# Moving each set of split activations to its own distance from the weights in the 512-byte block

## The chip, the cores and the metric

One core of one Trainium2 chip runs the whole program. The metric is the device time of one execution in microseconds (us); shorter is better.

## What is computed

Two transformer blocks over 256 tokens of width 1024, in float32. The first: a modulated norm, a mixer (retention heads and differential attention over the tokens and 256 context tokens), and a feed-forward layer that picks 16 single-neuron experts out of 16384 for each of 8 heads. The second: a short convolution mixer, attention to 256 memory tokens, a gated feed-forward layer (2 x 2816 columns up, 2816 rows down), shared keys and values, block attention, attention to memory again, a second feed-forward layer, and a last norm. Cut to the order of the second block:

```python
x = x + short_conv_mixer(h, conv_w_in[l], conv_w[l], conv_w_out[l])       # layer 0
x = x + moba_attention(h, moba_w_q[j], moba_w_o[j], cos, sin, k_blk, ...) # layer 1
x = x + mem_cross_attention(rms_norm_2(x, norm_mem[l]), ...)              # both layers
x = x + swiglu(rms_norm_2(x, norm_ffn[l]), ffn_w_gu[l], ffn_w_down[l])    # both layers
```

Nearly all of the work is products of the 256 tokens with large weight matrices that are each read once from memory.

## The kernel before, in words

**Tiles.** Activations lie transposed: 128 partitions hold 128 of the 1024 columns, a tile has 8 chunks (k) of 256 tokens, so 1024 bytes a chunk and partition. A weight block is 128 x 1024 float32, 512 bytes for each of eight 128 x 128 pieces. Every product of two float32 matrices is made of three float32r products: each factor is split into a high part and a low part (`whi`, `wlo` for weights in `split_w`, L113; `hh`, `hl` and their like for activations), and `mm3` (L134) multiplies high by high, low by high and high by low. For one output of 128 x 256 that is a run of 24 matmuls: eight pieces of `whi` with the high activations, eight of `wlo` with the high activations, eight of `whi` with the low activations. Before each matmul TensorE loads its 128 x 128 weights; the load of the next weights goes on while the matmul before streams its 256 tokens.

**Where things lie.** `placed` (L103) makes a tile with some room and returns a view that starts `at` elements into it. The values of `at` (16, 32, 40, 48) differ because the tiles start at different addresses. In the allocation of this kernel the three `whi` and two `wlo` buffers start at byte 224 of a 512-byte block, and so does every weight piece; all the sets that the change touches start at byte 416, which is 192 bytes further on, high and low alike. The memory sets (`hmh`, `hml` of `mem_kv`, L1001) of the second block's filler and the mixer's `hh`, `hl` (L455) are not made by `placed`: they start at byte 224, distance 0; the filler's set in the mixer starts at 256. In `mem_attn(0)` the turned probabilities `pTh`, `pTl` start at 384 and the memory values that are loaded for them at 256. Below, the distance of a matmul is the start of the operand that is streamed less the start of the operand that is loaded, modulo 512 bytes; where the activations are loaded and the weights streamed (`natural_steps`), 192 becomes 320.

**Stages.** `mixer` (0 to 288 us of the trace), then `peer`: 16 query blocks and 128 expert blocks with the set `h2h`, `h2l` (292 to 762), then the expert outputs (772 to 1120, with operands that the change leaves alone), then `conv_mixer`, `mem_attn(0)`, `swiglu(0)`, `moba`, `mem_attn(1)`, `swiglu(1)` and `finish`. SyncE's queue fetches the weight blocks in order, ScalarE makes the high part, VectorE or GpSimd the low part, TensorE multiplies; all orders are fixed when the program is built. Blocks of the filler (`fill` banks) are put between the blocks of other stages by hand (`PLACES`).

**Names.** `gained` (L264) makes a scaled set `hh`, `hl` for `mem_attn`, `conv_mixer`, `swiglu` and `moba`; `cat` is the set that a stage's last projection reads (`oh`/`ol`, `ch`/`cl`); `act` is `fh`/`fl`, 22 chunks; `hq` is moba's query set. The values in `moba` come from `natural_steps` (L166), where the activations are the loaded weights and the weights stream.

Of the kernel before, what the change touches and what calls it, by code (L numbers as in the profile page):

```python
# [28 lines left out]
KC = 8  # L29
EPS = 1e-6  # L30
NCH = 128
NKC_FF = 22
# [33 lines left out]
LOWEST = -3.0e38  # L66

ROOM = 128
G_NORM1, G_NORM2, G_MIX, G_MEM, G_MEMKV, G_FFN, G_KV, G_FINAL = 0, 1, 2, 4, 6, 8, 10, 11


class Build:
# [188 lines left out]
            nc.vector.scalar_tensor_tensor(h[1][:, k, cols], t, Bv[:, k:k + 1],  # L261
                                           h[0][:, k, cols].bitcast(F32), op0=OP.add, op1=OP.subtract)

    def gained(self, pool, x, gi, name="h", at=40):  # L264

        hi = self.placed(pool, name + "h", at, tag=name + "h", bufs=1)
        lo = self.placed(pool, name + "l", at, tag=name + "l", bufs=1)
        for k in range(KC):
            self.gain_chunk(x[:, k], gi, k, hi[:, k], lo[:, k])
        return hi, lo  # L270
# [441 lines left out]
    def peer(self):  # L712
        nc, io = self.nc, self.io
        with ExitStack() as ctx:
            self.banks(ctx, "peer")
            big = self.pool(ctx, "slots")
            pool = self.pool(ctx, "peer")
            slots = big.tile([P, NCH, T], F32, name="slots")
            h = self.placed(pool, "h2h", 48), self.placed(pool, "h2l", 48)
            space = slots[:, FREE:, :].rearrange("p c t -> p (c t)")  # L720
            at = [0]

# [190 lines left out]
            for cp in range(NCH // 2):  # L913
                self.lo_plan = UPLAN if cp < R1 else GPLAN
                o = self.psum([P, 2, T])
# [23 lines left out]
            pool = self.pool(ctx, "experts")  # L939
# [189 lines left out]
    def mem_attn(self, l, kv):  # L1129
        nc, io = self.nc, self.io  # L1130
        with ExitStack() as ctx:
            pool = self.pool(ctx, f"mem{l}")
            kT, v = kv
            h = self.gained(pool, self.x, G_MEM + l)
            cat = self.placed(pool, "oh", 40), self.placed(pool, "ol", 40)
            r = None

            def query(hd):
                nonlocal r
                o = self.psum([P, 2, T])  # L1140
                q = pool.tile([P, 2, T], F32, name="q", tag="q", bufs=1)
                qh, ql = (pool.tile([P, 2, T], F32R, name="q" + c, tag="q" + c, bufs=3) for c in "hl")
                for i in range(2):
                    self.block(o[:, i], io["mem_wq"][l, 2 * hd + i], h, late=hd == i == 0)
                if hd == 0:
                    r = self.tracked_norm(pool, "nr", tables=l == 0)
                nc.vector.scalar_tensor_tensor(q, o, 1.0 / 16.0, r[:, None, :].to_broadcast([P, 2, T]),
                                               op0=OP.mult, op1=OP.mult)
                nc.scalar.copy(qh, q)
                getattr(nc, QLO).tensor_sub(ql, q, qh)  # L1150
                return qh, ql

            def weigh(hd, q):
                ps = []
                for tt in range(2):
                    s = self.psum([P, T], "sc")
                    t = slice(tt * P, (tt + 1) * P)
                    self.mm3(s, [(q[0][:, i, t], q[1][:, i, t], kT[0][:, 2 * hd + i], kT[1][:, 2 * hd + i])
                                 for i in range(2)])
                    ps.append(self.softmax(pool, s, T, "ms"))  # L1160
                return ps

            def turned(ps):
                pT = [pool.tile([P, 2, 2, P], F32R, name="pT" + c, tag="pT" + c, bufs=2) for c in "hl"]
                for tt, p in enumerate(ps):
                    tr = self.psum([P, 2, P], "aux")
                    for j in range(2):
                        nc.tensor.transpose(tr[:, j], p[:, j * P:(j + 1) * P], self.ident)
                    nc.scalar.copy(pT[0][:, :, tt], tr)
                    nc.vector.tensor_sub(pT[1][:, :, tt], tr, pT[0][:, :, tt])  # L1170
                return pT

            def apply(hd, pT):
                o = self.psum([P, 2, T], "aux")
                for i in range(2):
                    c = slice((2 * hd + i) * P, (2 * hd + i + 1) * P)
                    self.mm3(o[:, i], [(v[0][:, j, c], v[1][:, j, c], pT[0][:, j], pT[1][:, j]) for j in range(2)])
                nc.scalar.copy(cat[0][:, 2 * hd:2 * hd + 2], o)
                nc.vector.tensor_sub(cat[1][:, 2 * hd:2 * hd + 2], o, cat[0][:, 2 * hd:2 * hd + 2])

            self.at(f"m{l}")
            qs = [query(0), query(1)]
            self.at(f"mq{l}")
            ps = weigh(0, qs[0])
            for hd in range(3):
                if hd < 2:
                    qs.append(query(hd + 2))
                self.at((f"mh{l}", hd))
                pT = turned(ps)
                ps = weigh(hd + 1, qs[hd + 1])  # L1190
                apply(hd, pT)
            self.at(f"me{l}")

            def rest():
                pT = turned(ps)
                yield
                apply(3, pT)

            self.residual_l(io["mem_wo"][l], cat, 6, rest())
# [27 lines left out]
    def conv_mixer(self, hook):  # L1227
        nc, io = self.nc, self.io
        with ExitStack() as ctx:
            pool = self.pool(ctx, "conv")  # L1230
            cw = self.load(pool, "conv_w", [P, KC, 3])
            h = self.gained(pool, self.x, G_MIX, at=16)
            cat = self.placed(pool, "ch", 16), self.placed(pool, "cl", 16)

            def gate(m, o, b):
                cu = pool.tile([P, 2, T], F32, name="cu", tag="cu", bufs=2)
                nc.vector.tensor_mul(cu, o, r[:, None, :].to_broadcast([P, 2, T]))
                z = pool.tile([P, T], F32, name="z", tag="z", bufs=2)
                nc.gpsimd.tensor_mul(z, cu[:, 0], cu[:, 1])
                y = pool.tile([P, T], F32, name="cy", tag="cy", bufs=2)  # L1240
                nc.vector.tensor_scalar(y, z, cw[:, m, 2:3], None, op0=OP.mult)
                nc.vector.scalar_tensor_tensor(y[:, 1:], z[:, :T - 1], cw[:, m, 1:2], y[:, 1:],
                                               op0=OP.mult, op1=OP.add)
                nc.vector.scalar_tensor_tensor(y[:, 2:], z[:, :T - 2], cw[:, m, 0:1], y[:, 2:],
                                               op0=OP.mult, op1=OP.add)
                nc.gpsimd.tensor_mul(y, y, r)
                t = pool.tile([P, T], F32, name="ct", tag="ct", bufs=2)
                nc.vector.tensor_mul(t, b, y)  # L1248
                nc.scalar.copy(cat[0][:, m], t)
                nc.vector.tensor_sub(cat[1][:, m], t, cat[0][:, m])  # L1250

            self.adder = getattr(nc, CADD)
            for k in range(KC):
                self.track(self.x[:, k], k)
            self.adder = nc.gpsimd
            for m in range(KC):
                self.at(("c", m))
                if m == HOOK:
                    hook()
                o = self.psum([P, 2, T], "sc" if m < 2 else "mm")  # L1260
                for i, c in enumerate((1, 2)):
                    self.block(o[:, i], io["conv_wi"][8 * c + m], h, late=m == i == 0)
                    if m == 1 and i == NORM1:
                        r = self.tracked_norm(pool, "nr", tables=True)
                b = self.psum([P, T])
                self.block(b, io["conv_wi"][m], h)
                if m == 0:
                    first = o, b
                    continue
                if m == 1:  # L1270
                    gate(0, *first)
                gate(m, o, b)
            self.at("ce")
            self.residual_l(io["conv_wo"], cat)

    def swiglu(self, l):
        nc, io = self.nc, self.io
        with ExitStack() as ctx:
            pool = self.pool(ctx, f"ffn{l}")
            h = self.gained(pool, self.x, G_FFN + l)  # L1280
            self.at(f"f{l}")
            act = self.placed(pool, "fh", 40, NKC_FF), self.placed(pool, "fl", 40, NKC_FF)
            for m in range(NKC_FF):
                o = self.psum([P, 2, T])
                for i in range(2):
# [12 lines left out]
            for m in range(KC):  # L1298
                o = self.psum([P, T])
                n = 0  # L1300
                while n < NKC_FF:
# [8 lines left out]
                    n = e  # L1310
# [33 lines left out]
    def moba(self):  # L1344
        nc, io = self.nc, self.io
        with ExitStack() as ctx:
            pool = self.pool(ctx, "moba")
            mask = self.load(pool, "causal", [P, 2, T])
            hk = self.gained(pool, self.x, G_KV)
            v = pool.tile([P, 2, 1024], F32, name="v")  # L1350
            r = rn = None
            waiting = []
# [28 lines left out]

            self.at("bk")
            kT = pool.tile([P, KC, T], F32, name="k")
            hq = [self.placed(pool, "hq" + c, 32) for c in "hl"]

            def query(hd):
                return plain(io["moba_wq"][hd], hq, 128.0 ** -0.5)
# [9 lines left out]
                ahead = t  # L1397
                self.gain_chunk(self.x[:, hd], G_MIX + 1, hd, hq[0][:, hd], hq[1][:, hd])

            cat = self.placed(pool, "oh", 32), self.placed(pool, "ol", 32)  # L1400

            def weigh(hd, q):
                ps = []
# [219 lines left out]
```

## Time and profile before

| | |
|---|---|
| median of 3 runs | 1889.74 us (1888.1 to 1890.78) |
| profiled execution | 1882.41 us, its span 1880.6 us |
| TensorE matmul busy | 1833.2 us, 97% of the span |
| VectorE, ScalarE, GpSimd busy | 70%, 52%, 24% |
| mean DMA rate | 178 GB/s |
| mean granted clock of TensorE | 0.992 |

The profile is that of one execution. Busy times of matmuls are modelled at their ends (a matmul's record is about 276 ns long although the next one starts after 113 ns), so the distance between starts is what counts: the chain in order of time gives a stretch and its matmuls, and the timeline gives the start of each run of eight.

### The profile page before, as it was taken

The numbers are of one execution on the slowest core, as the hardware profiler recorded it, in microseconds if no ns is written. First come the engines' busy times: TensorE is split into PE (matmuls) and PEld (weight loads), VectorE is DVE, ScalarE is ACT, GpSimd is POOL, SyncE is SP. The second block draws the span as 40 slices with busy tenths as digits, with TensorE's granted clock in tenths as the row PEclk, the third lists the DMA queues.
The fourth block names the chain that finished last, engine by engine and source line by source line (L and its number), as shares of the span: only waits on it lengthen the run. The fifth ranks groups of instructions, "written<-read, shape, count | busy, mean of one in ns | idle before, by whom it ended". The sixth has DMA issues, their size and how long they took to land.

```text
span 1880.6 us, 34809 instructions
## 1 busy us (share of the span) xinstructions
PE 1833.2 (97%) x13562; PEld 1717.2 (91%) x13562; DVE 1313.8 (70%) x2592; ACT 975.1 (52%) x1533; POOL 453.7 (24%) x254
## 2 busy tenths in 40 slices
PE   8999999999999999999999998999999999999997
PEld 6796888999999999788888878999999999999997
DVE  7879875995566676865555568777765679766654
ACT  7746335445555444445545555465554645555543
POOL 0001105787766777100000004112000111110001
PEclk9999999999999999999999999999999999999999
DMA  8763444454444444755555555544555553445553
GB/s 298 254 217 105 142 129 156 170 189 169 150 160 154 157 157 157 247 191 195 195 191 193 196 192 184 191 169 148 200 193 196 190 180 124 169 136 190 187 184 124
DMA packets 99765, 335.13 MB, mean 178 GB/s; under 512 B 12400, under 2 KB 13456, under 8 KB 99216
## 3 DMA queue, kind: packets, MB, share of 16 engines
q1 hardware_dynamic: 98160, 330.68, 51.0%
q8 instruction: 106, 1.74, 0.4%
q10 hardware_dynamic: 1440, 2.23, 0.3%
q14 instruction: 59, 0.48, 0.1%
HBM read 329.59 MB, written 3.28 MB: 177 GB/s over the span
## 4 chain that ended last, share of the span: by engine, by line
PE 87%; DVE 6%; DMA 3%; ACT 3%; issue 1%; POOL 0%; SPq 0%; DVEq 0%; ACTq 0%; POOLq 0%
PE mm L144 54%; PE pair L956 17%; PE mm L179 4%; PE pair L893 3%; PE fill L179 2%; DVE wlo L122 2%; PE fill L144 1%; PE sc L144 1%; DMA mraw<-w_mod 1%; PE aux L144 1%; DMA raw<-w_mod 1%; ACT whi L118 1%; DMA raw<-peer_v 0%; PE sc L628 0%; PE sc L554 0%
## 5 line engine op out<-in xcount | busy, mean ns | idle before, releaser
L118 ACT CAST whi<-raw 128x1024 fp32r<-128x1024 f32 x564 | 591.9, 1051 | 558.3 <-PE mm L144 280.4
L122 DVE TENSOR_TENSOR wlo<-raw,whi 128x1024 fp32r<-128x1024 f32 x420 | 526.7, 1255 | 298.7 <-PE pair L956 131.6
L122 POOL TENSOR_TENSOR wlo<-raw,whi 128x1024 fp32r<-128x1024 f32 x144 | 344.7, 2395 | 131.6 <-PE mm L144 113.6
L144 PE MATMUL mm<-hh,whi 128*128 128x256 f32 (+1 forms) x1184 | 178.2, 287 | 5.9 <-DVE ct L1248 5.1
L144 PE MATMUL mm<-hl,whi 128*128 128x256 f32 (+1 forms) x1184 | 174.5, 284 | 2.1 <-DVE hl L261 1.2
L144 PE MATMUL mm<-hh,wlo 128*128 128x256 f32 (+1 forms) x1184 | 175.9, 285 | 0.0
L144 PE MATMUL mm<-h2h,whi 128*128 128x256 f32 x1152 | 168.2, 289 | 4.1 <-ACT h2h L260 4.0
L226 POOL TENSOR_TENSOR acc<-acc,accsq 128x256 f32<-128x256 f32 x42 | 42.1, 1004 | 523.1 <-ACT accsq L224 523.1
L144 PEld LDWEIGHTS mm<-hh,whi 128*128 128x128 f32 x1184 | 155.4, 190 | 10.9 <-issue 7.6
L956 PE MATMUL pair<-whi,actl 128*128 128x512 f32 x512 | 158.6, 391 | 2.4 <-DVE actl L949 2.3
L956 PE MATMUL pair<-whi,acth 128*128 128x512 f32 x512 | 158.3, 390 | 0.3 <-ACT acth L948 0.2
L956 PE MATMUL pair<-wlo,acth 128*128 128x512 f32 x512 | 157.8, 389 | 0.7 <-DVE wlo L122 0.7
L144 PEld LDWEIGHTS mm<-hl,whi 128*128 128x128 f32 x1184 | 153.5, 189 | 5.0 <-DVE hl L261 1.7
L144 PEld LDWEIGHTS mm<-hh,wlo 128*128 128x128 f32 x1184 | 154.6, 190 | 3.5 <-issue 1.5
L144 PE MATMUL mm<-h2h,wlo 128*128 128x256 f32 x1152 | 157.5, 279 | 0.0
L144 PE MATMUL mm<-h2l,whi 128*128 128x256 f32 x1152 | 157.1, 279 | 0.0
L144 PEld LDWEIGHTS mm<-h2h,whi 128*128 128x128 f32 x1152 | 147.4, 192 | 5.0 <-ACT h2h L260 4.8
L144 PEld LDWEIGHTS mm<-h2h,wlo 128*128 128x128 f32 x1152 | 144.6, 189 | 0.0
L144 PEld LDWEIGHTS mm<-h2l,whi 128*128 128x128 f32 x1152 | 144.0, 189 | 0.0
L956 PEld LDWEIGHTS pair<-whi,actl 128*128 128x128 f32 x512 | 95.4, 188 | 24.4 <-DVE actl L949 5.0
L956 PEld LDWEIGHTS pair<-wlo,acth 128*128 128x128 f32 x512 | 96.0, 188 | 21.3 <-DVE wlo L122 1.1
L956 PEld LDWEIGHTS pair<-whi,acth 128*128 128x128 f32 x512 | 95.5, 188 | 20.9 <-ACT acth L948 1.5
(407 smaller groups left out, 3062.7 us busy)
## 6 DMA issues: line engine op xcount, KB each, us to landing
raw<-peer_u SPq DMA_DIRECT2D x128, 512.0 KB, 3.5
raw<-peer_v SPq DMA_DIRECT2D x128, 512.0 KB, 3.5
raw<-ffn_gu SPq DMA_DIRECT2D x88, 512.0 KB, 4.3
raw<-ffn_dn SPq DMA_DIRECT2D x44, 512.0 KB, 3.9
raw<-w_mod SPq DMA_DIRECT2D x64, 256.0 KB, 3.8
raw<-conv_wi SPq DMA_DIRECT2D x24, 512.0 KB, 3.5
raw<-mem_wk SPq DMA_DIRECT2D x16, 512.0 KB, 4.5
mraw<-w_mod SPq DMA_DIRECT2D x16, 512.0 KB, 6.2
```

What stands on the lines that cost most here:

```text
L118: self.hi_copy = nc.scalar.copy(hi, raw)
L122: (nc.vector if plan == "v" else nc.gpsimd).tensor_sub(lo, raw, hi)
L144: self.matmul = nc.tensor.matmul(out, a, b, start=first and j == 0, stop=last and j == 3 * n - 1)
L179: self.matmul = nc.tensor.matmul(outs[i // 2][:, i % 2], a[:, k, :], b[:, w], start=k == 0 and s == 0 and i % 2 == 0, stop=k == 7 and s == ...
L226: self.adder.tensor_add(self.acc, self.acc, self.last)
L893: nc.tensor.matmul(o[:, 2 * j + i], A[:, i], Bt[:, i], start=True, stop=True)
L956: nc.tensor.matmul(acc[th][:, dh], x[:, tsl], wt[:, dh * 512:dh * 512 + 512], start=c == 0 and s == 0, stop=c == NCH - 1 and s == 2)
```

## The change

A table `SHIFT` gives each set a shift in bytes for its high and its low part, and `shifted` puts both `placed` views that much further on in tiles of the same size. Nothing else differs: the same instructions on the same shapes in the same order, on other addresses.

```diff
+SHIFT = {"h2": (16, -16), "conv": (32, 64), "c": (96, 160), "mem0": (8, -8), "o0": (-96, 192), "ffn0": (48, -48),
+         "f0": (20, -20), "kv": (256, 224), "hq": (24, -24), "o": (4, -4), "mem1": (80, -80), "o1": (112, -112),
+         "ffn1": (40, -40), "f1": (12, -12)}
...
-    def gained(self, pool, x, gi, name="h", at=40):
+    def shifted(self, pool, names, what, at, k=KC, room=ROOM):
 
-        hi = self.placed(pool, name + "h", at, tag=name + "h", bufs=1)
-        lo = self.placed(pool, name + "l", at, tag=name + "l", bufs=1)
+        return tuple(self.placed(pool, n, at + d // 4, k, room, tag=n, bufs=1) for n, d in zip(names, SHIFT[what]))
+
+    def gained(self, pool, x, gi, name="h", at=40, what=None):
+
+        hi, lo = self.shifted(pool, (name + "h", name + "l"), what, at)
...
-            h = self.placed(pool, "h2h", 48), self.placed(pool, "h2l", 48)
+            h = self.shifted(pool, ("h2h", "h2l"), "h2", 48)
...
-            h = self.gained(pool, self.x, G_MEM + l)
-            cat = self.placed(pool, "oh", 40), self.placed(pool, "ol", 40)
+            h = self.gained(pool, self.x, G_MEM + l, what=f"mem{l}")
+            cat = self.shifted(pool, ("oh", "ol"), f"o{l}", 40)
...
-            h = self.gained(pool, self.x, G_MIX, at=16)
-            cat = self.placed(pool, "ch", 16), self.placed(pool, "cl", 16)
+            h = self.gained(pool, self.x, G_MIX, at=16, what="conv")
+            cat = self.shifted(pool, ("ch", "cl"), "c", 16)
...
-            h = self.gained(pool, self.x, G_FFN + l)
+            h = self.gained(pool, self.x, G_FFN + l, what=f"ffn{l}")
...
-            act = self.placed(pool, "fh", 40, NKC_FF), self.placed(pool, "fl", 40, NKC_FF)
+            act = self.shifted(pool, ("fh", "fl"), f"f{l}", 40, NKC_FF)
...
-            hk = self.gained(pool, self.x, G_KV)
+            hk = self.gained(pool, self.x, G_KV, what="kv")
...
-            hq = [self.placed(pool, "hq" + c, 32) for c in "hl"]
+            hq = self.shifted(pool, ("hqh", "hql"), "hq", 32)
...
-            cat = self.placed(pool, "oh", 32), self.placed(pool, "ol", 32)
+            cat = self.shifted(pool, ("oh", "ol"), "o", 32)
```

With the 192 bytes of before, the distances from the weights in the 512-byte block become, high and low: h2 208 and 176; conv 224 and 256; c 288 and 352; mem0 200 and 184; o0 96 and 384; ffn0 240 and 144; f0 212 and 172; kv 448 and 416; hq 216 and 168; o 196 and 188; mem1 272 and 112; o1 304 and 80; ffn1 232 and 152; f1 204 and 180.

## Rows read from the trace of the kernel before

**Rows 1.** The page: engine rows, busy tenths in 40 slices, granted clock.

```profile
PE 1833.2 (97%) x13562; PEld 1717.2 (91%) x13562; DVE 1313.8 (70%) x2592; ACT 975.1 (52%) x1533; POOL 453.7 (24%) x254
...
PE   8999999999999999999999998999999999999997
...
PEclk9999999999999999999999999999999999999999
...
PE 87%; DVE 6%; DMA 3%; ACT 3%; issue 1%; POOL 0%; SPq 0%; DVEq 0%; ACTq 0%; POOLq 0%
```

**Rows 2.** The chain in order of time, its longest pieces: start, length, what.

```profile
347.84 90.34 PE mm L144 x767
827.36 289.96 PE pair L956 x1278
1185.30 24.50 PE mm L144 x216
1313.58 174.10 PE mm L144 x1536
1687.90 180.92 PE mm L144 x1536
```

**Rows 3.** Windows: length, busy of PE, PEld, DVE, ACT, POOL, clock, DMA.

```profile
350.00:430.00 80.00, 80.00 (x681) 80.00 (x680) 77.35 (x310) 37.76 (x43) 68.20 (x29) 1.00 0.54 184
1313.00:1428.00 115.00, 115.00 (x1015) 114.95 (x1014) 80.93 (x111) 61.67 (x88) 0.00 (x0) 1.00 0.58 199
1688.00:1806.00 118.00, 118.00 (x1005) 118.00 (x1004) 80.39 (x109) 60.97 (x87) 0.00 (x0) 1.00 0.55 187
```

**Rows 4.** The page's costliest groups: the set of the expert blocks.

```profile
L144 PE MATMUL mm<-h2h,wlo 128*128 128x256 f32 x1152 | 157.5, 279 | 0.0
L144 PE MATMUL mm<-h2l,whi 128*128 128x256 f32 x1152 | 157.1, 279 | 0.0
```

**Rows 5.** The tile `hh` in 1313 to 1428 us: durations min/median/max.

```profile
L144 PEld LDWEIGHTS mm<-hh,wlo x336: 187/188/188, 1314.2 to 1426.5; 128*128 128x128 f32 x168
L144 PE MATMUL mm<-hh,wlo x336: 276/276/277, 1314.3 to 1426.7; 128*128 128x256 f32 x168
```

**Rows 6.** The tile `hh` in 1688 to 1806 us: durations min/median/max.

```profile
L144 PE MATMUL mm<-hh,wlo x336: 281/281/282, 1688.7 to 1805.4; 128*128 128x256 f32 x168
L144 PEld LDWEIGHTS mm<-hh,whi x334: 187/188/193, 1687.9 to 1804.3; 128*128 128x128 f32 x167
```

**Rows 7.** The tile `hmh` in 1163 to 1310 us: durations min/median/max.

```profile
L144 PEld LDWEIGHTS fill<-hmh,wlo x64: 187/192/193, 1163.1 to 1306.1; 128*128 128x128 f32 x64
L144 PE MATMUL fill<-hmh,wlo x64: 274/283/287, 1163.2 to 1306.2; 128*128 128x256 f32 x64
```

**Rows 8.** Timeline of TensorE, 1182 to 1189 us: start, length, what, count.

```profile
1182.28 1.10 PE L144 MATMUL fill<-hmh,whi 128*128 128x256 f32 x8
1183.22 1.12 PE L144 MATMUL fill<-hmh,wlo 128*128 128x256 f32 x8
1184.18 1.12 PE L144 MATMUL fill<-hml,whi 128*128 128x256 f32 x8
1185.14 1.09 PE L144 MATMUL mm<-hh,whi 128*128 128x256 f32 x8
1186.06 1.07 PE L144 MATMUL mm<-hh,wlo 128*128 128x256 f32 x8
1186.97 1.07 PE L144 MATMUL mm<-hl,whi 128*128 128x256 f32 x8
```

**Rows 9.** Timeline of TensorE, 336.5 to 345 us: two query blocks.

```profile
337.13 1.19 PE L144 MATMUL mm<-h2h,whi 128*128 128x256 f32 x8
...
340.05 0.61 PE L753 MATMUL pair<-slots 128*128 128x128 f32 x4
340.41 1.17 PE L144 MATMUL mm<-h2h,whi 128*128 128x256 f32 x8
...
343.23 0.60 PE L753 MATMUL pair<-slots 128*128 128x128 f32 x4
```

**Rows 10.** Timeline of TensorE, 26.5 to 29.2 us: distance 32 from `whi`.

```profile
27.33 1.10 PE L144 MATMUL fill<-hmh,wlo 128*128 128x256 f32 x8
28.27 1.09 PE L144 MATMUL fill<-hml,whi 128*128 128x256 f32 x8
```

**Rows 11.** Timeline of TensorE, 256 to 257.5 us: 14 matmuls between these, distance 480.

```profile
255.81 0.28 PE L179 MATMUL fill<-whi,hmh 128*128 128x256 f32 x1
...
257.47 0.28 PE L179 MATMUL fill<-wlo,hmh 128*128 128x256 f32 x1
```

**Rows 12.** Timeline of TensorE, 1282.9 to 1284.5 us: 12 matmuls, distance 128.

```profile
1282.99 0.40 PE L144 MATMUL aux<-pTh,memv0h 128*128 128x256 f32 x2
...
1284.43 0.28 PE L144 MATMUL mm<-oh,whi 128*128 128x256 f32 x1
```

**Rows 13.** Timeline of TensorE, 1493.9 to 1499 us: moba's values, 44 matmuls, distance 320.

```profile
1493.82 0.28 PE L179 MATMUL mm<-whi,hh 128*128 128x256 f32 x1
...
1499.00 0.28 PE L179 MATMUL mm<-wlo,hh 128*128 128x256 f32 x1
```

## Prediction

> **What bounds the kernel now.** The page's engine rows come first: TensorE's matmuls are busy in 97% of the span, in every slice 80% or more, at full clock, and 87% of the chain that ends last is TensorE [rows 1]. VectorE, at 70%, is next. So the span is matmul starts laid end to end, and the view to read is the chain in order of time, which gives long stretches without a wait. Two of them are the same work, gate, up and down of the two feed-forward layers, 1536 matmuls each: 174.10 us in layer 0, 180.92 us in layer 1 [rows 2]. Per matmul that is 113.3 and 117.8 ns. The windows show both with TensorE busy throughout, granted clock 1.00 and nothing waited for [rows 3], so neither clock nor supply makes the difference; and both sets lie at the same distance, 192 bytes. The expert blocks show the same two rhythms: 767 matmuls in 90.34 us, 117.8 ns [rows 2], and two neighbouring query blocks of 24 that take 2.92 and 2.82 us from their first matmul to the next foreign one [rows 9], 0.10 us or 24 x 4.2 ns apart. I call them the short and the long rhythm. A stretch keeps its rhythm until something interrupts it.
>
> The tile views give a cause, if not a law. In the short rhythm a weight load takes 188 ns in median and never more than 188 in the row shown, a matmul 276 [rows 5]; in the slow one some loads last 193, and the matmul 281 [rows 6]; in the filler's blocks at distance 0 the load's median is 192 and the matmul's 283 [rows 7], and starts are (1185.14 - 1183.22)/16 = 120.0 ns apart [rows 8]. So the load of the next weights and the stream of the present activations get in each other's way, and addresses can change how often. Other distances: 32 gives 0.94/8 = 117.5 ns [rows 10], 480 gives 1.66/14 = 118.6 [rows 11], 128 gives 1.44/12 = 120.0 [rows 12], 320 gives 5.18/44 = 117.7 [rows 13]. Only 192 shows 113.3 anywhere.
>
> **The change, part by part.** No instruction is added or removed, the DMAs and waits are those of before, and ScalarE and VectorE write the same shapes. With 97% busy TensorE and VectorE 70% at most in the span [rows 1], nothing else is late if TensorE gains or loses 1%; in the feed-forward window VectorE has 81 of 115 us [rows 3]. So each nanosecond per matmul counts in full. 8928 matmuls read moved sets.
>
> *Sets moved by 32 bytes or more.* ffn0 and ffn1 (1056 matmuls each), conv (576), c, o0, o1, mem1 (192 each), kv (384). The nearest rows to their new distances lie between 117.5 and 120.0 [rows 10 to 13]; I take 118, near the lower end, because some of the unknown distances (64, 448) may behave as 192 does. ffn0 loses 1056 x 4.7 = 5.0 us, conv 576 x 4.5 = 2.6, c, o0 and o1 together 576 x 4.3 = 2.5, mem1 about 0.5 (it is mixed now), kv's keys 0.9; ffn1 has the long rhythm already and loses 0.2, kv's values likewise nothing. Sum +11.7. Bounds: all of them short, -5.9 (ffn1 gains 4.7); all at 120.0, +19.2.
>
> *Sets moved by 24 bytes or less.* h2 (3456), f0 and f1 (528 each), o, mem0, hq (192 each): 5088 matmuls, at 208 to 216 and 168 to 188 or nearer to 192. h2's mean record of 279 [rows 4], between 276 and 281, says three fifths long now, 116.0 ns; f0 is short and f1 long [rows 2]. I take their shares of short and long as they are, 0 us. Bounds: all short -13.3 (h2 -9.5, f1 -2.3, o, hq and mem0 -1.5), all long +9.2 (h2 +5.9, f0 +2.3, the rest +1.0).
>
> *High and low apart.* Before, distance is the same through a block. After it, each block changes distance twice, after 16 matmuls and after 24. The nearest row is the step from the filler's 0 to 192: the first eight take 0.92 us, the next 0.91 [rows 8], where eight in the short rhythm take 0.907: 0.013 us. 5088/24 = 212 blocks of the near sets, two steps each, 0.013 at most: 5.5 us; a step of 8 to 48 bytes is smaller than one of 192, so I take half, +3 (bounds 0 and 5.5; for the far sets it is within the price of 118, which comes from short runs).
>
> Sum: 11.7 + 0 + 3 = +14.7 us on the profiled execution's 1882.4, which makes 1897. That execution is 7.3 us below the median of the runs, 1889.7. A feed-forward stage in the other rhythm is worth 6.8 us [rows 2], so the timed runs may just have had other shares; then the surplus is not to be added again, since the far sets have no short rhythm left to lose. If it is a fixed surplus, 1904. I say 1898.
>
> The Trainium skill's page "SBUF — State Buffer" (section "Who interferes with whom") speaks against any effect: TensorE has two independent read ports, for the moving operand and for weight loads, and "PE and ACT never wait on anyone". By it only addresses change and the sum is 0; rows 5 to 8 disagree, with 188 against 192 ns for a load and 113.3 against 120.0 ns a matmul at full clock.
>
> **The rivals.** *Faster: the steps shake off the long rhythm.* After each of eight filler blocks (between 1163 and 1618 us), where the distance changes from 0 to 192 without a pause, the stream goes into the short rhythm; one is in rows 8, and the 216 matmuls behind it take 113.4 ns each [rows 2]. Interrupted streams take either rhythm [rows 9]. If every step of distance throws the stream into the short rhythm, and the new distances have one, the long stretches go: -5.9 - 13.3 = -19.2, and 372 blocks x 2 steps x 0.013 = 9.7 come back at most: 1863 to 1873 on the profiled execution, 1870 to 1880 with its 7.3 us, some 1876. It decides once about half of the blocks, h2's above all, come out at 113.3. Against it: five other distances show no stretch at 113 ns [rows 10 to 13, 8].
>
> *Same.* Either addresses matter no more than a throw of the rhythm (h2's share falls a little, ffn1 gains what ffn0 loses), or the views land elsewhere than the shifts say because the tiles move: 1886 to 1893, about 1890.
>
> *Much slower: everything at the price of distance 0.* 120.0 everywhere: far +19.2; near h2 3456 x 4.0 = 13.8, the rest 7.1: +40, 1922. It needs what rows 12 show at 128 to hold for 168 to 216 too.
>
> **How the numbers follow.** Forecast 0.50 (1898, own range 1892 to 1906), faster 0.22 (1876), same 0.20 (1890), much slower 0.08 (1922). About 0.2%, 3.8 us, is what a measurement of this kernel can tell from no change. Faster 0.22, same 0.20, slower 0.58. The range reaches over the faster case's time and past the forecast's fixed surplus of 7 us and the far sets at 120: 1876 to 1915; outside are the much slower case and the better part of the faster one.
>
> **What would show it.** In the chain in order of time: layer 0's feed-forward stretch of 1536 near 179 us instead of 174.10, layer 1's near 181 or, in the faster rival, 175. The tile view of `h2l` and `h2h`: means of 279 if the shares hold, 277 in the faster rival, 283 in the much slower one. Weight loads with a median of 189 or more in ffn0 would show the collisions. The prediction is wrong if ffn0 stays at 113 ns a matmul, or if h2's 3456 matmuls leave 116 ns by more than 2 ns either way; ScalarE, VectorE and the DMA rows should stand as they are.

## The result and the profile after

The changed kernel takes 1909.31 us (median of four runs, 1908.04 to 1910.2) where the kernel before took 1890.05 beside it: a ratio of 1.0103, 95% interval 1.0085 to 1.012. It is slower by 19.3 us; 8.3 were forecast. The direction and the range held, the size did not. One of the ten timed runs of a later kernel, the one with its halves 256 bytes apart, took 1946.82 us at a granted clock of 0.901 instead of 0.99 and is left out of its numbers.

The page of the changed kernel answers [rows 1]: busy times and instruction counts of each engine.

```profile
span 1907.4 us, 34809 instructions
PE 1862.7 (98%) x13562; PEld 1747.0 (92%) x13562; DVE 1313.7 (69%) x2592; ACT 973.0 (51%) x1533; POOL 448.8 (24%) x254
...
PEclk9999999999999999999999999999999999999999
```

The same 13562 matmuls are busy 29.5 us longer, at the same granted clock, and VectorE and ScalarE stand where they stood. So the time is made in TensorE itself. The chain in order of time (start, length, what) says where:

```profile
348.40 90.24 PE mm L147 x767
835.28 290.00 PE pair L962 x1278
1195.07 25.62 PE mm L147 x216
1327.16 181.75 PE mm L147 x1536
1711.03 184.53 PE mm L147 x1536
```

Set the starts beside those of [rows 2]: the delay is 0.56 us at the first piece, 7.92 at the second, 9.77 at the third, 13.58 where the first feed-forward stage starts, 23.13 where the second does, and 26.74 at the end of that. (The profiled execution before took 1882.4 us and this one 1909.14, hence 26.7 and not 19.3.) So the expert blocks lose 7.4 us, what follows `pair` 1.9, conv and the memory 3.8, the first feed-forward stage 7.65, what stands between the two stages 1.9, the second stage 3.6. Per matmul the two stages went from 113.3 and 117.8 ns to 118.3 and 120.1. The 290 us of `pair`, whose operands were not moved, are the same to 0.04.

The windows (length, busy of PE, PEld, DVE, ACT, POOL with their counts, clock, DMA share, GB/s) of the first two answer [rows 3]:

```profile
1327.00:1442.00 115.00, 115.00 (x982) 115.00 (x981) 79.59 (x108) 60.09 (x86) 0.00 (x0) 1.00 0.55 190
1711.00:1829.00 118.00, 118.00 (x979) 118.00 (x978) 78.76 (x107) 59.74 (x86) 0.00 (x0) 1.00 0.53 182
```

TensorE is busy throughout and at full clock as before, and gets through 982 matmuls instead of 1015, and 979 instead of 1005. The page's groups of the expert blocks answer [rows 4] (total us, mean ns), and the timeline answers [rows 9] (start, length, what):

```profile
L147 PE MATMUL mm<-h2l,whi 128*128 128x256 f32 x1152 | 160.7, 282 | 0.0
L147 PE MATMUL mm<-h2h,wlo 128*128 128x256 f32 x1152 | 160.3, 282 | 0.0
```

```profile
337.53 1.20 PE L147 MATMUL mm<-h2h,whi 128*128 128x256 f32 x8
...
340.47 0.60 PE L759 MATMUL pair<-slots 128*128 128x128 f32 x4
340.83 1.20 PE L147 MATMUL mm<-h2h,whi 128*128 128x256 f32 x8
...
343.77 0.60 PE L759 MATMUL pair<-slots 128*128 128x128 f32 x4
```

From the first matmul to the next foreign one both query blocks take 2.94 us. Before, one took 2.92 and the other 2.82. Neither is short now.

One table serves all that follows. A set's *cadence* is the mean time from the start of one of its matmuls to the start of the next, in ns, worked out from the trace's records; those over 130 ns, with a wait or another shape behind them, are left out. Cost is the difference times the set's matmuls.

| set (matmuls) | distance, high / low | cadence before | after, high / low | cost, us | forecast |
|---|---|---|---|---|---|
| h2 (3456) | 208 / 176 | 116.2 | 118.6 / 119.2 | 9.0 | 0 |
| f0 (528) | 212 / 172 | 113.3 | 120.4 / 120.3 | 3.7 | 0 |
| f1 (528) | 204 / 180 | 117.8 | 118.2 / 120.0 | 0.6 | 0 |
| mem0, hq, o (576) | 168 to 216 | 115 to 117.7 | 120.2 to 121.3 | 2.7 | 0 |
| ffn0 (1056) | 240 / 144 | 113.5 | 117.4 / 116.9 | 4.0 | 5.0 |
| conv (576) | 224 / 256 | 113.6 | 118.4 / 119.0 | 2.9 | 2.6 |
| c, o0, o1 (576) | 80 to 384 | 113.6 to 113.9 | 117.6 to 119.6 | 2.9 | 2.5 |
| mem1, kv (576) | 64 to 448 | 115, 113.4, 117.8 | 113.9 to 118.4 | 0.7 | 1.4 |
| ffn1 (1056) | 232 / 152 | 117.7 | 121.0 / 120.4 | 3.3 | 0.2 |

The far sets cost 13.8 us (11.7 forecast), the near ones 16.0 (0 forecast). Together that is 29.8, 3 more than the executions differ by. Most of the 3 came back in the pauses that a cadence leaves out: the intervals over 130 ns, all of them together, are 2.6 us shorter than before.

### The profile page after: what moved, and what is told of

Its sections match the earlier page's. It is cut to its first block, busy times and chain, and to the rows that moved or that the text cites. A ratio compares the mean times of both kernels' runs of the same rounds, so it can differ in the third digit from the quotient of the medians.

```text
span 1907.4 us, 34809 instructions
## 1 busy us (share of the span) xinstructions
PE 1862.7 (98%) x13562; PEld 1747.0 (92%) x13562; DVE 1313.7 (69%) x2592; ACT 973.0 (51%) x1533; POOL 448.8 (24%) x254
## 4 chain that ended last, share of the span: by engine, by line
PE 88%; DVE 6%; ACT 2%; DMA 2%; issue 1%; SPq 0%; POOL 0%; DVEq 0%; ACTq 0%; POOLq 0%
PE mm L147 55%; PE pair L962 17%; PE mm L182 4%; PE pair L899 3%; PE fill L182 2%; DVE wlo L125 2%; PE fill L147 1%; PE sc L147 1%; DMA mraw<-w_mod 1%; PE aux L147 1%; DMA raw<-peer_v 1%; DMA raw<-w_mod 0%; DVE roper L399 0%; PE sc L634 0%; PE sc L560 0%
## 5 line engine op out<-in xcount | busy, mean ns | idle before, releaser
L147 PE MATMUL mm<-hl,whi 128*128 128x256 f32 (+1 forms) x1184 | 178.9, 288 | 1.7 <-DVE hl L264 1.2
L229 POOL TENSOR_TENSOR acc<-acc,accsq 128x256 f32<-128x256 f32 x42 | 37.5, 893 | 541.1 <-ACT accsq L227 541.1
L883 DVE TENSOR_TENSOR ohA<-fill,selT 128x256 f32<-128x256 f32 x128 | 53.7, 419 | 93.1 <-PE pair L899 89.8
```

Of the source, the lines that this page charges most:

```text
L147: self.matmul = nc.tensor.matmul(out, a, b, start=first and j == 0, stop=last and j == 3 * n - 1)
L229: self.adder.tensor_add(self.acc, self.acc, self.last)
L883: nc.vector.tensor_tensor(A, iota[:, None, :].to_broadcast([P, 2, P]), selT[:, 1, t:t + 2, None].to_broadcast([P, 2, P]), op=OP.is_equal)
```

## The experiments

Two questions were open. Does a set pay because its halves lie apart (a step in every block), or for the distance of each half? And by what rule of the distance, that 16 bytes cost as much as 48? The first four kernels ran beside a single run of the kernel before, 1880.75 us, which is lower than any of the 23 runs of it further down; so their times are set against the medians. Where no ratio is given, the kernel ran once. Only addresses differ in any of them. Distances are given modulo 512 unless said otherwise.

### High and low at the same place

The low half of every set is moved as its high half is.

```
SHIFT = {"h2": (16, 16), "conv": (32, 32), "c": (96, 96), "mem0": (8, 8), "o0": (-96, -96), "ffn0": (48, 48),
         "f0": (20, 20), "kv": (256, 256), "hq": (24, 24), "o": (4, 4), "mem1": (80, 80), "o1": (112, 112),
         "ffn1": (40, 40), "f1": (12, 12)}
```

> Each low part at the shift of its high part: every set at one distance again, that of the change's high part. In the changed kernel h2h (208) takes 118.6 ns a matmul and h2l (176) 119.2, ffn0's stretch of 1536 takes 181.75 us and ffn1's 184.53. Theory 1, the step between high and low throws the streams out: without a step the 113.3 rhythm comes back wherever a set has one, h2 falls to 116 ns, ffn0's stretch to 174 to 177, the time to 1885 to 1892. Theory 2, a set's own distance sets its rhythm: h2h stays at 118 to 119 and h2l joins it, ffn0's stretch stays at 180 to 183, ffn1's at 183 to 186, the time at 1905 to 1912.

It took 1911.52 us. Its chain, the same pieces as above:

```profile
348.81 91.39 PE mm L145 x767
...
1327.90 181.45 PE mm L145 x1536
1711.97 185.94 PE mm L145 x1536
```

No step is left inside a block, and nothing is gained. Most cadences are near those of the high halves in the table: h2 119.2 (at 208), ffn0 117.2 (240), f0 120.0 (212), f1 118.2 (204), conv 118.3 (224). Two sets are dearer with their halves together than the high half was in the changed kernel: ffn1 (232) with 122.4 against 121.0, and o (196) with 123.0 against 121.3. So it is not the lying apart that costs. Each set pays for its own distances, and where the other half lies shifts a half's price by 1 to 2 ns at most here.

### The near sets back

The six sets that the prediction priced at nothing go back to 192, the others stay moved.

```
"h2": (0, 0), "f0": (0, 0), "f1": (0, 0), "o": (0, 0), "mem0": (0, 0), "hq": (0, 0)
```

> h2, f0, f1, o, mem0 and hq back at 192, the sets moved by 32 bytes or more stay moved. By the rhythms read in the changed kernel the near sets cost 16 us of its 26.7 over the profiled execution of before (h2 9.0, f0 3.7, mem0 1.1, hq 1.0, o 0.7, f1 0.6). Theory 2: the time falls to 1892 to 1897, h2 back to 116 ns. Rival: the restarts that the moved sets cause elsewhere keep h2 in the 117.8 rhythm, then h2 alone costs 5.5 more and the time is 1898 to 1902. The prediction's far sum was +11.7, which would be 1894.

It took 1896.05 us, 13.3 less than the changed kernel. Chain, and the group of the expert blocks:

```profile
347.79 86.95 PE mm L145 x767
...
1316.74 180.39 PE mm L145 x1536
1698.43 184.00 PE mm L145 x1536
```

```profile
L145 PE MATMUL mm<-h2l,whi 128*128 128x256 f32 x1152 | 155.9, 278 | 0.0
```

h2 is at 115.1 (116.2 in the kernel before), and the piece of 767 at 113.4 each, the short rhythm, where it took 117.8 before and 117.7 in the changed kernel. What is left is 1896.05 - 1890.05 = 6 us over the median of before, and 13.6 over its profiled execution, which had the short rhythm in ffn0 and f0. So the near sets carry some 13 us. That is one run, with its own share of the rhythms: against the kernel before, h2 stood 1.1 ns shorter here and f0, at 117.8, 4.5 longer. ffn1 (232 / 152) is at 121.0 and 120.4 here too, with f1 behind it back at 117.8: its price did not follow its neighbour's place.

### Small steps

```
"h2": (4, 4), "ffn0": (8, 8), "ffn1": (16, 16), "f0": (32, 32), "f1": (24, 24), "conv": (64, 64), "c": (48, 48),
"mem1": (32, 32), "o1": (16, 16), and (0, 0) for mem0, o0, kv, hq and o
```

> High and low together, one shift for each set: h2 4 bytes, ffn0 8, ffn1 16, f0 32, f1 24, conv 64, c 48, mem1 32, o1 16; the others at 192. Theory 3, lines of 16 bytes: a start off a multiple of 16 costs a matmul 120 ns or more, so h2 (4), ffn0 (8) and f1 (24) come out at 120 to 121, ffn1, f0, c, mem1, o1 (multiples of 16) at 117 to 118. Theory 4, only the distance modulo 128 counts and a few bytes do nothing: h2 and ffn0 as before (113.3 or 117.8), f0 and mem1 (distance 224, which is 96 modulo 128) 117 to 118, conv (256, which is 0) 120. By theory 3 the time is about 1882 plus 14 (h2) plus 7 (ffn0), some 1905 to 1912; by theory 4 1885 to 1895.

It took 1922.63 us, the slowest of these four, and more than either theory gave (1905 to 1912, 1885 to 1895). Chain:

```profile
349.73 94.58 PE mm L145 x767
...
1338.85 185.11 PE mm L145 x1536
1725.24 183.80 PE mm L145 x1536
```

The smallest steps cost the most. By cadence: 4 bytes (h2) 122.7 and 123.5, 8 bytes (ffn0) 121.6, 24 bytes (f1) 120.6; 16 bytes (ffn1, o1) 119.1 and 119.0, 32 bytes (f0, mem1) 118.4 and 118.3, 48 bytes (c) 117.2, and 64 bytes (conv, distance 256) 119.9. The prediction's picture, in which a small step stays near what 192 does, is the wrong way round. The dearest are those off a multiple of 16 bytes, as theory 3 had it, only by more than its 120 to 121; f1 at 204 in the first kernel, 118.2, is the exception.

### Steps of 128

```
"h2": (128, 128), "ffn0": (256, 256), "ffn1": (-128, -128), "f0": (128, 128), "f1": (256, 256), "conv": (128, 128),
"c": (256, 256), "mem0": (-128, -128), "o0": (128, 128), "kv": (256, 256), "hq": (128, 128), "o": (256, 256),
"mem1": (128, 128), "o1": (256, 256)
```

> High and low together, every set moved by a multiple of 128 bytes: to 320 (h2, f0, conv, o0, mem1, hq), 448 (ffn0, c, f1, kv, o, o1) or 64 (ffn1, mem0). Theory 4, the distance modulo 128 decides: all streams show 113.3 or 117.8 and nothing else, the two feed-forward stretches of 1536 take 174.1 or 180.9 us or a mix of both, the time is 1875 to 1900. Rival, only 192 has a 113.3 rhythm: all at 117.5 to 120, feed-forward stretches 181 to 184 us, the time 1902 to 1912.

It took 1895.47 us, inside theory 4's range. Chain:

```profile
347.30 86.93 PE mm L145 x767
...
1318.49 180.91 PE mm L145 x1536
1700.95 180.92 PE mm L145 x1536
```

Every set, at 64, 320 or 448, shows one of two cadences: 113.4 (c and kv's keys at 448, the 767 of h2 above) or 117.7 to 117.9 (ffn0 at 448, ffn1 at 64, conv and f0 at 320, f1 at 448), or, as h2 in the whole with 116.7, a mixture of them. Those are the two rhythms of the kernel before. So 192 is one of four places, those whose distance is 64 modulo 128; at 64 itself (ffn1, mem0) only the long one was seen. This one execution happened to have the long rhythm in both stages, at 180.9 as ffn1 has it in [rows 2].

### The distance, or where the stream starts

The distance and the start of the streamed operand moved together so far. Here the high halves of the weights start 4 bytes further on, and h2, conv, c, f0 and ffn1 too.

```
+    hi = pool.tile([P, w + 32 * own], F32R, name=pre + "hi", tag=pre + "hi", bufs=3)[:, own:own + w]
     SHIFT: (4, 4) for h2, conv, c, f0, ffn1; (0, 0) for all others
```

> Only addresses differ from the kernel before: the high halves of the weights start 4 bytes further on (their low halves do not), and the sets h2, conv, c, f0 and ffn1 start 4 bytes further on too; all other sets stay. So in h2 and ffn1 the products with a high weight have their two operands at the distance of before (64 modulo 128) with both starts 4 bytes off a multiple of 16, and the products with a low weight are at 68 with only the streamed start off. In ffn0 and f1 the products with a high weight are at 60 with only the loaded start off, and those with a low weight are at 64 with both starts on. Theory A (the distance between the two starts counts, wherever they lie): h2 with high weights 113.3 to 117.8 ns from start to start, h2 with low weights 120 to 123.5; ffn0 with high weights 120 to 123.5, with low weights 113.3 to 118; time some 1903 to 1912 us, since about half of the products are off. Theory B (a streamed operand that starts off a multiple of 16 bytes costs, whatever the weights do): h2 and ffn1 at 120 to 123.5 ns with both halves of the weights, ffn0 and f1 at 113.3 to 118 with both; 1915 us or so. Theory C (a loaded operand that starts off costs): every product with a high weight at 120 or more, with low weights at 113 to 118, in all sets; 1912 to 1920 us.

It took 1927.7 us. First the chain's `pair` piece, then its tile rows (durations min/median/max). In these products the weights are the streamed operand, and their high half alone starts 4 bytes off a multiple of 16.

```profile
843.65 299.76 PE pair L961 x1278
```

```profile
L961 PE MATMUL pair<-whi,acth x512: 389/398/504, 779.5 to 1144.1; 128*128 128x512 f32 x171
...
L961 PE MATMUL pair<-whi,actl x512: 392/402/503, 780.0 to 1144.9; 128*128 128x512 f32 x171
...
L961 PE MATMUL pair<-wlo,acth x512: 387/389/403, 780.4 to 1145.3; 128*128 128x512 f32 x171
```

Where another kernel's chain shows that piece whole, it takes 290.0 to 290.3 us, and in every other kernel all three groups have a median of 389. One of them in the kernel before:

```profile
L956 PE MATMUL pair<-whi,actl x512: 388/389/501, 763.0 to 1118.8; 128*128 128x512 f32 x171
```

Here the two groups with the displaced stream are at 398 and 402, the third, between them on the same engine, stays at 389. Two thirds of 1278 times 11 ns is 9.4 of the 9.8 us. No theory had counted this piece; it is most of the way from theory B's 1915 to 1927.7.

Most 256-wide products agree. h2, conv, c, f0 and ffn1 stream from 4 bytes off and cost 120.3 to 120.9 with the high weights, although the distance is 64 modulo 128, and 121.4 to 121.7 with the low ones at 68. ffn0 and f1 stream from a multiple of 16; they cost 117.9 to 118.3 with the displaced high weights, and 115.5 to 116.1 with the low ones at 64. Theory A falls, and theory B holds for these sets: a streamed start off a multiple of 16 bytes costs, whatever the distance; a loaded one costs 2 ns or so. It does not hold everywhere: in moba's values, where the weights stream and the loaded activations did not move, the products took 117.5 to 118.0 ns in the kernel before; here they take 119.3 and 120.1 with the displaced high weights, but 119.8 with the low ones too, which start on a multiple of 16.

### Halves 256 apart

```
SHIFT: (0, 256) for every set
```

> Every set's high half stands where it stood before (distance 192) and every low half 256 bytes further (448), so a step of 256 bytes comes with each block, but both distances are 64 modulo 128. If only the remainder modulo 128 counts and a step within it does nothing: the two rhythms of before, 113.3 or 117.8 ns for a whole stage, and 1880 to 1891 us. The rival that a step throws the stream out of the long rhythm into the short one: both feed-forward stages and the experts' stage at 113.3 to 113.5 ns, 1872 to 1878 us. The rival that the remainder modulo 256 or 512 counts too, or that each step costs on its own: the low halves' products at 118 ns or more and 1894 to 1900 us.

The ratio is 0.9992 (0.9979 to 1.0006), medians 1888.29 (nine runs) and 1889.34. Chain of the profiled execution:

```profile
348.32 90.34 PE mm L145 x767
...
1317.48 180.91 PE mm L145 x1536
1699.14 180.92 PE mm L145 x1536
```

ffn0's high half is at 117.63 and its low half, 256 bytes further, at 117.64. Steps between good places cost nothing that shows, and they do not shake off the long rhythm either: the prediction's faster rival is out, in the one form in which it could be tried without leaving the good places. The 23 runs of before, beside this kernel and the next, range from 1880.99 to 1893.42 us, and ffn0, short in [rows 2], is long here at the same addresses of its high half. That looks as if the rhythm were drawn anew in each run; two traces of one and the same kernel, which would show it, are not there.

### The sets that the change leaves alone

All moved sets stand at 192, and the mixer's and the memory's activations (at 0 and 32 until now) are brought there.

```
-            h = (pool.tile([P, KC, 2 * T], F32R, name="hh"), pool.tile([P, KC, 2 * T], F32R, name="hl"))
+            h = [pool.tile([P, KC * 2 * T + ROOM], F32R, name="h" + c)[:, 48:48 + KC * 2 * T].rearrange(
+                "p (k t) -> p k t", k=KC) for c in "hl"]
-        hm = [pool.tile([P, KC, T], F32R, name="hm" + c, tag="hm" + c, bufs=1) for c in "hl"]
+        hm = [self.placed(pool, "hm" + c, (40, 48)[l], tag="hm" + c, bufs=1) for c in "hl"]
```

> All sets that the change moved stand where they stood in the kernel before (distance 192). What is moved instead are the three sets that the change leaves alone: the mixer's activations from distance 0 to 192 (some 1250 products, of which half have the weights as streamed operand), and the memory's activations of both layers from 32 and 0 to 192. They ran at 117 to 120 ns from start to start. If the remainder 64 modulo 128 is the place without a surcharge: these go to 113.3 or 117.8 ns, 2 to 8 us less than the kernel before, 1880 to 1887 us by the median, and the mixer's products show nearly none of 119 ns or more. If the surcharge at 0 came from these stages' other work (the normalisation beside them) and not from the addresses: no change, 1887 to 1891 us, the same 119 to 120 ns. If the step from 0 to 192 at the two ends of the fillers is what set the rhythm of the experts' stage, that stage goes as a whole to 113.3 ns (under 83 us for the chain's 767 products in place of 90) and the time under 1880 us.

The ratio is 0.9998 (0.9985 to 1.0011), medians 1888.84 and 1889.34. The filler's block answers [rows 8] (timeline: start, length, what):

```profile
1181.34 1.07 PE L145 MATMUL fill<-hmh,whi 128*128 128x256 f32 x8
1182.24 1.07 PE L145 MATMUL fill<-hmh,wlo 128*128 128x256 f32 x8
1183.15 1.07 PE L145 MATMUL fill<-hml,whi 128*128 128x256 f32 x8
1184.06 1.07 PE L145 MATMUL mm<-hh,whi 128*128 128x256 f32 x8
```

The filler went from 120.0 ns to (1184.06 - 1181.34)/24 = 113.3, the mixer's products of 256 columns from 119.7 to between 116.5 and 117.9. The surcharge at 0 is the address's. In the mixer's value products the weights stream from where they did, and only the loaded activations moved: 119.9 became 117.8. So the place of the loaded operand counts too, and not that of the streamed one alone. The mixer's products of 512 columns went the other way, from some 230 ns at 0 to 233.5 at 192. By cadence all of it together is some 3 us; the mixer's own output set fell into the long rhythm, 117.8 for 115.2, and takes 0.5 back. The 2 to 8 us expected do not show in the time: the interval, -2.8 to +2.1 us, neither shows nor excludes the rest. The experts' piece of 767 stays at 90.34 us, so it did not go short for want of a step at the fillers. It is no version to recommend over the kernel before on these numbers.

### h2 alone

```
"h2": (16, -16), and (0, 0) for all others
```

> Of the change only the set h2 moves (its high half 16 bytes up to distance 208, its low half 16 down to 176); all other sets stand as in the kernel before. If each set pays for its own distance: h2's products at 118.6 (high) and 119.2 ns (low) as in the changed kernel, all others at 113.3 to 117.8 as before; 3456 times 2.6 ns, so 9 us: 1898 us by the median, ratio 1.004 to 1.006. If h2's surcharge needs the other sets off their place too: h2 at 116.2 and 1888 to 1891 us. If a step of 16 bytes in one stage also sets the rhythm of the stages behind it: both feed-forward stages at a rhythm that is neither 113.3 nor 117.8 ns.

The ratio is 1.0027 (1.0004 to 1.005): 1894.18 beside 1889.71. Chain and group:

```profile
835.12 289.99 PE pair L960 x1278
...
1322.39 180.91 PE mm L145 x1536
1704.36 174.11 PE mm L145 x1536
```

```profile
L145 PE MATMUL mm<-h2l,whi 128*128 128x256 f32 x1152 | 160.7, 282 | 0.0
```

h2's cadences are 118.6 and 119.2, to the tenth those of the changed kernel, and `pair` starts at 835.12 where it starts at 835.28 there and at 827.36 in [rows 2]. So h2 pays alone, some 8 us by this piece. The two profiled executions, this one and that before, each have one feed-forward stage short and one long (here ffn1 is the short one, 174.11), and differ by 9.7 us, 1892.1 and 1882.41; 9 were expected. The ratio's 5 us (0.8 to 9.4) is under that and under the 1.004 expected; the five runs span 11.4 us, and whether it was their rhythms is not shown.

### The other end, remainder 0

All sets at distances that are multiples of 128, spread over the four.

```
"h2": (-64, -64), "ffn0": (64, 64), "ffn1": (-64, -64), "f0": (192, 192), "f1": (320, 320), "conv": (64, 64),
"c": (192, 192), "mem0": (64, 64), "o0": (-64, -64), "kv": (64, 64), "hq": (-64, -64), "o": (192, 192),
"mem1": (64, 64), "o1": (-64, -64)
```

> Every set's two halves together at a multiple of 128 from the weights, the remainder 0, and the sets spread over all four such places of a block of 512: h2, ffn1, o0, o1 and hq at 128, ffn0, conv, kv, mem0 and mem1 at 256, f0, c and o at 384, f1 at 0. If the remainder modulo 128 is what counts, on multiples of 16: all four places alike, 119.5 to 120.5 ns per product, no 113.3 anywhere in them; h2 3456 times 3.8 ns and the other 5472 times some 3.5 ns over the kernel before, 13 and 19 us, 1918 to 1924 us. If the period is 256 or 512 and 0 alone is bad: 128 and 384, or 256, at 113.3 to 117.8 ns, under 1910 us. If only a start off a multiple of 16 bytes costs and multiples are free but for chance: 1880 to 1891 us.

It took 1914.25 us, less than the 1918 to 1924 expected. Chain, and the tile `hh` in ffn0 (distance 256) and in ffn1 (128), durations min/median/max:

```profile
1331.96 183.61 PE mm L145 x1536
1717.69 182.97 PE mm L145 x1536
```

```profile
L145 PEld LDWEIGHTS mm<-hh,whi x280: 192/192/192, 1340.3 to 1439.1; 128*128 128x128 f32 x140
L145 PE MATMUL mm<-hh,whi x280: 283/283/283, 1340.4 to 1439.2; 128*128 128x256 f32 x140
```

```profile
L145 PE MATMUL mm<-hh,whi x318: 279/281/285, 1717.8 to 1829.4; 128*128 128x256 f32 x159
L145 PEld LDWEIGHTS mm<-hh,wlo x317: 187/188/189, 1718.4 to 1829.9; 128*128 128x128 f32 x159
```

At 256 every load takes 192 and every matmul 283, so 120.0 a matmul (ffn0, conv, kv, and f1 at 0). At 128 and 384 ffn1, f0, c, o and o1 run at 118.6 to 118.8, a mixture, h2 at 119.6 to 119.7 and o0 at 119.7 to 120.2. So no place of remainder 0 has either rhythm of 64 for a whole set; but 128 and 256 are not quite alike, and the remainder modulo 128 is not the whole rule.

## Why the prediction was right or wrong

*What bounds the kernel* held. Nothing but TensorE moved, and nearly every nanosecond of cadence showed in the span, 26.7 of 29.8 us.

*Far sets*: +11.7 forecast, 13.8 measured. The price of 118 from the rows at 32, 128, 320 and 480 fits ffn0 (5.0 against 4.0), conv (2.6 against 2.9) and c, o0 and o1 (2.5 against 2.9). It fails at ffn1: 0.2 forecast, since that set already had the long rhythm, and 3.3 measured, because 232 and 152 are off a multiple of 16 and cost 120.4 to 121.0.

*Near sets* is the step that failed: "I take their shares of short and long as they are, 0 us", with +9.2 as the upper bound. They measured +16.0 by cadence, 9.0 of it h2's, and the kernel with the near sets back puts them at 13.3. The long rhythm was taken for the worst that a place near 192 can do. But a few bytes are not near, in two ways. h2's places, 208 and 176, are multiples of 16 and lose both rhythms by leaving the remainder 64: 118.6 and 119.2, alone as well as with the others. The other near sets, 7.0 us together, are off a multiple of 16, and the small steps show such places at 122.7 to 123.5 (4 bytes) and 121.6 (8), dearer than the distance 0 that the prediction held for the top at 120.0. The rows before could not show the second: all distances read there are multiples of 16. A hint of the first was there: 192, where both rhythms were seen, and 320, at the long one's 117.7, have the remainder 64 modulo 128, and the others have 0, 32 and 96. The prediction named the sign itself: h2 leaving 116 ns by more than 2; it left by 2.6.

*High and low apart*: +3 forecast; no such cost was found. Together took 1911.52 against 1909.31, with ffn1 and o dearer and not cheaper, and at good places 256 apart the ratio is 0.9992.

*The surplus of 7.3 us* was rightly not added. The changed kernel's profiled execution, 1909.14, stands at its median, 1909.31, where that of the kernel before stood 7.6 us below its own; hence 19.3 us against the median and 26.7 between the profiled executions. The reason given, that moved sets have no short rhythm left to draw, fits the table, where only kv's keys are still near it, but the spread of the runs does not show it: four runs of the changed kernel span 2.2 us, the four of the kernel before beside them 2.7, and only its 23 later ones 12.4.

So the sum by the median was 11.7 + 0 + 3 - 7.3, with a point added for the doubt, and would have been 13.8 + 16.0 + 0 - 3 - 7.3 = 19.5 with what was measured. The 3 here is what was left over between cadence and span, so that this sum comes out is no test of its terms. That 1909 lies inside the range is luck: the upper end stood for a fixed surplus and far sets at 120, and neither came.

*What would show it*: ffn0's stretch was to be near 179 us (it is 181.75) and ffn1's near 181 (184.53), h2's means 279 or 283 (282). Loads in ffn0 were to have a median of 189 or more: they have 188, at most 191, with ffn0 at 117.

```profile
L147 PEld LDWEIGHTS mm<-hh,wlo x328: 187/188/191, 1327.8 to 1441.2; 128*128 128x128 f32 x164
```

Medians of 190 to 192 stand where a matmul costs 120 and more: 190 and 191 in the changed kernel's f0 and ffn1, 192 at the remainder 0 shown above. A load's median tells the dear places from the others, not 113 from 117.

*The rivals*: faster is out (no step shook off a rhythm), and so is same. Much slower, 1922 with everything at 120.0, was nearer in its mechanism than the forecast: the near sets did reach 118.6 to 121.3, while the far ones stayed mostly under 119. The rule of the Trainium skill's page "SBUF — State Buffer" (section "Who interferes with whom"), that TensorE's two read ports are independent, gave 0. The traces disagree with that sum by 26.7 us, and the `pair` rows above do once more: 398 and 402 ns against 389 by an address alone. Whether one port waits for the other, or an operand's own reads take longer from such a place, is not settled; the mixer's value products, where only the loaded operand moved, speak for more than the streamed one.

What stays open: why one place has two rhythms, what draws them, why 204 is cheap among those off 16 bytes, why moba's values do not split by the streamed start, which place is good for 512 columns, and what in the memory has a period of 128 with a trace of 256.

## What to carry to other kernels

Where a stage is matmul starts laid end to end, the relative place of streamed and loaded operand is worth up to 9% of it (113.3 to 123.5 ns here, for 256 columns), and "a little off" is not "nearly the same": keep streamed operands at multiples of 16 bytes, and look for the good remainder by trying several in one run, since each set shows its own price. Price an unknown place by the worst one in the trace or above, not by the rhythm that the good place happens to have. And before a sum is made on a profiled execution, see whether it stands at the median of its runs, and whether the change takes that luck away.

## What the runs showed of the hardware

- For a 128x256 float32r product at granted clock 1.00, by distance between the two starts (streamed minus loaded): 64 modulo 128 gives 113.3 or 117.8 ns, or a mixture (at 64 itself only 117.8 was seen); on other multiples of 16 the remainder 16 gives 116.4 to 117.6, 112 117.1 to 117.8, 32 117.4 to 117.9, 48 118.3 to 119.2, 80 118.6 to 119.2, 96 118.3 to 120.0, and 0 119.0 to 120.1 (at 0 and 256) or 118.5 to 120.2 (at 128 and 384).
- Off a multiple of 16 bytes: 4 bytes over 192 gives 121.2 to 123.5, 8 bytes 120.2 to 121.6, 20 and 24 bytes 120.0 to 120.8, 40 bytes 121.0 to 122.4, but 12 bytes 118.2 to 118.4; 4 to 40 bytes under it 120.0 to 121.1. Where activations stream, the streamed start counts for more than the distance: 120.3 to 120.9 with both operands 4 bytes off. Moba's values, where weights stream, do not show it.
- For a 128x512 product a streamed start 4 bytes off costs 9 to 13 ns in the record (389 to 398 and 402). Which place is good is not the same as for 256 columns: in the mixer 0 gave some 230 ns from start to start and 192 gave 233.5.
- A place of remainder 64 has both rhythms at identical addresses and clock, 174.1 and 180.9 us for the same 1536 matmuls (layer 0's stage in the kernel before and with h2 alone moved), and both stages kept theirs to the end. Runs of one kernel differ by 0.66%; one such stage is worth 0.36%. No set of 256-wide products at another place shows the short rhythm as a whole.
